# The last layer's gate of an encoder kernel: two blocks of tokens against three, with reloaded weights in another order

## The chip, the cores and the metric

The kernel runs on one core of a Trainium2 chip. The metric is the device time of one execution in microseconds. The engines are named as the profile names them: PE is TensorE (PEld its weight loads), DVE is VectorE, ACT is ScalarE, POOL is GpSimd, and SP issues most DMAs. A line number such as L834 is a line of the kernel before; from line 818 on the changed kernel's numbers are up to two higher.

## What is computed

The reference is a two-layer encoder trunk on 1024 tokens of width 1024. The change touches only the end of the second layer and the final norm:

```python
h = h + jnp.concatenate([y_mla, y_gla], axis=-1) @ w_out[i]
gate = jax.nn.sigmoid(rmsnorm(h, ple_norm[i]) @ w_ple_gate[i])
h = h + gate * (p[i] @ w_ple_proj[i])
...
return rmsnorm(h, final_norm)
```

`rmsnorm` divides by the root of the mean square over the 1024 channels of a token, so the final output of a token needs all channels of its h.

## The kernel before

Activations lie with channels on the 128 partitions and tokens along the row, so h is eight tiles `hs[t]` of 128 channels by 1024 tokens. Every fp32 product is made of three matmuls on split operands (high part times high part, low times high, high times low). The order of the instructions on each engine is fixed at build time by a scheduler; each engine runs its queue in that order and waits where an operand or a buffer is not ready.

**Weights.** `load_split` (L135) brings one half tile (128 x 512) of a weight: SP loads it into `wr` (two buffers), ACT copies it to the high part (L142) and its negative to the low part (L146), and POOL issues a second, accumulating DMA (L147) of the same half onto the low part. `load_w8` (L150) does this for the two halves of one output tile. Its results go to the `wh`/`wl` buffers, five halves of each, or, with `keep`, to tiles `kwh`/`kwl` of their own.

**The gate of the last layer** (L804 to L859) runs over blocks of tokens, `TAIL`, 736 and then 288 tokens. For each block it makes the eight output tiles t one after another. A tile is 24 matmuls for each of its `k` column pieces (L834), into a PSUM tile of tag `mm` or `aux` in turn (two buffers each); then DVE multiplies by `r_h`, the rstd of the gate's norm (L837), ACT takes the sigmoid (L838), SP loads `pj`, the tile of the projected embedding (L840), DVE multiplies by it (L841) and adds the product to h (L843), ACT squares h (L847, or L845 into `acc` for the first tile), and DVE adds the square to `acc` (L849). The weights of tiles 4 to 7 (`KEEP`) are kept from the first block on; those of tiles 0 to 3 are loaded again for the second block, whose order is 0, 1, 2, 3, 4, 5, 6, 7.

**The final norm.** After a block, `rstd` (L170) sums `acc` over the partitions: the split parts `sqh` (ACT, L128) and `sql` (DVE, L129) go through two matmuls with ones (L181), DVE transposes the result (L184), makes the inverse root with small operations (L189 to L197) and transposes back (L201). Then `finish` (L808) scales a tile of h by it (L811) and SP stores it (L812). For the first block the eight finishes are put into `later` and made one after each tile of the second block, through a buffer `fin`; for the last block they stand at the end, in place. `gt` and `fin` share three buffers.

Of the kernel before, what the change touches and what calls it, by code (L numbers as in the profile page):

```python
# [31 lines left out]

T_SMALL, T_GQ, T_GK, T_GV, T_CKV, T_CQ, T_GG, T_GA = 0, 1, 3, 5, 9, 11, 14, 18
N_IN = 22
TAIL = (slice(0, 736), slice(736, 1024))

KEEP = (4, 5, 6, 7)

# [19 lines left out]
def hybrid_encoder(ctx: ExitStack, tc: tile.TileContext, xT, pT, pos, vecs, w_in, wq, wk, wv,  # L58
# [35 lines left out]
    def bank2(tag="mm"):  # L94
        return pp.tile([P, 2, HC], F32, tag=tag, name="ps")

    def on(site):
        return {"P": nc.gpsimd, "V": nc.vector}[ENG[site]]
# [15 lines left out]
    def flat(t):  # L114
        return t.rearrange("p a b -> p (a b)")

    def st(shape=(P, S), dt=F32, name="st"):
        return sp.tile(list(shape), dt, tag="st", name=name)

    def mt(dt=F32, name="mt"):  # L120
        return rp.tile([P, S], dt, tag="r", name=name)
# [9 lines left out]
    def split_gain(hi, lo, src, g):  # L131
        nc.scalar.activation(hi, src, AF.Copy, scale=g)
        nc.vector.scalar_tensor_tensor(lo, src, g, hi.bitcast(F32), op0=ALU.mult, op1=ALU.subtract)
# [16 lines left out]
    def load_w8(src, keep=False):  # L150

        ops = []
        if keep:
            whole = mt(F32R, "kwh"), mt(F32R, "kwl")
        for half in range(2):
            c = slice(half * HC, (half + 1) * HC)
            hi, lo = load_split(src[:, c], HC, [t[:, c] for t in whole] if keep else None)
            ops += [(hi[:, k * P:(k + 1) * P], lo[:, k * P:(k + 1) * P]) for k in range(4)]
        return ops

    def mm3(ps, ws, xs):

        n = len(ws)
        for i, ((wh, wl), (xh, xl)) in enumerate(zip(ws, xs)):
            for j, (a, b) in enumerate(((wh, xh), (wl, xh), (wh, xl))):
                for c in range(2):
                    nc.tensor.matmul(ps[:, c, :], lhsT=a, rhs=b[:, c * HC:(c + 1) * HC],  # L167
                                     start=(i == 0 and j == 0), stop=(i == n - 1 and j == 2))
# [119 lines left out]
    for L in range(DEPTH):  # L288
# [496 lines left out]
        if not last_layer:  # L785
            xs = []
            sq = SquareSum()
            for t in range(8):
                ps = bank2()
                mm3(ps, load_w8(w_gate[L, t]), gh)  # L790
                g = st(name="gt")
                nc.vector.tensor_tensor(g, flat(ps), r_h, op=ALU.mult)
                nc.scalar.activation(g, g, AF.Sigmoid)
                pj = st(name="pj")
                nc.sync.dma_start(pj, projd[L][t])
                on("gate").tensor_tensor(g, g, pj, op=ALU.mult)
                on("hadd").tensor_tensor(hs[t], hs[t], g, op=ALU.add)
                nc.sync.dma_start(h1d[t], hs[t])
                sq.add(hs[t])
                hi, lo = mt(F32R, "xh"), mt(F32R, "xl")  # L800
                g1 = vec[:, V_LAYER * (L + 1) + V_LN + t:V_LAYER * (L + 1) + V_LN + t + 1]
                split_gain(hi, lo, hs[t], g1)
                xs.append((hi, lo))
        else:  # L804

            kept, later = {}, []

            def finish(t, w, r, o=None):  # L808
                hw = hs[t][:, w]
                o = hw if o is None else o[:, :w.stop - w.start]  # L810
                nc.vector.scalar_tensor_tensor(o, hw, vec[:, V_FIN + t:V_FIN + t + 1], r, op0=ALU.mult, op1=ALU.mult)  # L811
                nc.sync.dma_start(outT[t][:, w], o)  # L812

            for w in TAIL:
                n = w.stop - w.start
                k = -(-n // HC)
                m = n // k

                def cut(t):
                    return t.rearrange("p (c m) -> p c m", m=m)  # L820

                last_block = w.stop == S
                acc = mt(name="acc")[:, :n]
                todo = [t for t in range(8) if t not in kept] + list(kept)
                for at, t in enumerate(todo):
                    ps = bank2("aux" if at % 2 else "mm")[:, :k, :m]
                    ws = kept[t] if t in kept else load_w8(w_gate[L, t], t in KEEP)
                    if t in KEEP:
                        kept[t] = ws
                    for i in range(8):  # L830
                        for j, (a, b) in enumerate(((ws[i][0], gh[i][0]), (ws[i][1], gh[i][0]),
                                                    (ws[i][0], gh[i][1]))):
                            for c in range(k):
                                nc.tensor.matmul(ps[:, c, :], lhsT=a, rhs=cut(b[:, w])[:, c, :],  # L834
                                                 start=(i == 0 and j == 0), stop=(i == 7 and j == 2))
                    g = st(name="gt")[:, :n]
                    nc.vector.tensor_tensor(cut(g), ps, cut(r_h[:, w]), op=ALU.mult)  # L837
                    nc.scalar.activation(g, g, AF.Sigmoid)  # L838
                    pj = mt(name="pj")[:, :n]
                    nc.sync.dma_start(pj, projd[L][t][:, w])  # L840
                    nc.vector.tensor_tensor(g, g, pj, op=ALU.mult)  # L841
                    hw = hs[t][:, w]
                    nc.vector.tensor_tensor(hw, hw, g, op=ALU.add)  # L843
                    if at == 0:
                        nc.scalar.activation(acc, hw, AF.Square)  # L845
                    else:
                        nc.scalar.activation(g, hw, AF.Square)  # L847
                        if at < 7 or not last_block:
                            nc.vector.tensor_tensor(acc, acc, g, op=ALU.add)  # L849

                    if later:
                        finish(*later.pop(0), st(name="fin"))
                if last_block:
                    r = rstd((acc, g), D, n=n)
                    for t in todo:
                        finish(t, w, r[:, :n])
                else:
                    r = rstd(acc, D, n=n)
                    later = [(t, w, r[:, :n]) for t in todo]  # L859
# [82 lines left out]
```

## Time and profile before

| | |
|---|---|
| median of 3 runs | 1467.03 us (1465.24 to 1467.93) |
| profiled execution, its own time | 1462.53 us |
| its span, first to last instruction | 1460.8 us |
| mean granted TensorE clock, of full speed | 0.981 |
| PE busy | 1379.5 us, 94% |
| DVE busy | 863.2 us, 59% |
| ACT busy | 720.7 us, 49% |
| POOL busy | 427.7 us, 29% |

The busy shares are means over the whole program. The gate of the last layer fills the last 120 us of the span, from about 1341 us on, and is best read there by windows and timelines. Matmuls overlap: the time that one takes from the next is the distance of their starts, not the duration in its row.

### The profile page before, as it was taken

The numbers are of one execution on the slowest core, as the hardware profiler recorded it, in microseconds if no ns is written. First come the engines' busy times: TensorE is split into PE (matmuls) and PEld (weight loads), VectorE is DVE, ScalarE is ACT, GpSimd is POOL, SyncE is SP. The second block draws the span as 40 slices with busy tenths as digits, with TensorE's granted clock in tenths as the row PEclk, the third lists the DMA queues.
The fourth block names the chain that finished last, engine by engine and source line by source line (L and its number), as shares of the span: only waits on it lengthen the run. The fifth ranks groups of instructions, "written<-read, shape, count | busy, mean of one in ns | idle before, by whom it ended". The sixth has DMA issues, their size and how long they took to land. (4 is left out here: it accounts for less than half of the span.)

```text
span 1460.8 us, 21130 instructions
## 1 busy us (share of the span) xinstructions
PE 1379.5 (94%) x8400; PEld 1168.7 (80%) x8400; DVE 863.2 (59%) x1260; ACT 720.7 (49%) x1013; POOL 427.7 (29%) x312
## 2 busy tenths in 40 slices
PE   7999999999889999999999999889989999999985
PEld 6799778878678788888889877778877888878984
DVE  2576745788446544464455676667744564456547
ACT  6565475545345443364445555534444453346541
POOL 3421211212346454112432111211244564311210
PEclk9999999999999999999999999999999999999997
DMA  7663546345531223256765343334651212335863
GB/s 275 184 131 73 108 106 178 82 100 132 151 61 54 65 73 88 71 108 151 200 163 124 79 88 79 88 74 94 176 144 41 66 51 73 101 80 101 218 135 123
DMA packets 77794, 163.94 MB, mean 112 GB/s; under 512 B 9536, under 2 KB 17088, under 8 KB 77696
## 3 DMA queue, kind: packets, MB, share of 16 engines
q1 hardware_dynamic: 51200, 116.19, 26.0%
q0 software_dynamic: 26496, 46.41, 19.1%
q8 instruction: 66, 1.08, 0.3%
q14 instruction: 32, 0.26, 0.1%
HBM read 128.74 MB, written 25.43 MB: 106 GB/s over the span
## 5 line engine op out<-in xcount | busy, mean ns | idle before, releaser
L146 ACT ACTIVATE wl<-wr 128x512 fp32r<-128x512 f32 (+2 forms) x176 | 107.3, 610 | 311.5 <-PE ps L167 279.3
L675 POOL TENSOR_SCALAR sc<-sc,sums 128x1024 f32<-128x1024 f32 x64 | 182.0, 2856 | 101.7 <-DVE sums L674 83.7
L147 POOL DMA_DIRECT2D wl<-in_w_in x84 | 72.6, 877 | 349.1 <-ACT wl L146 311.3
L142 ACT ACTIVATE wh<-wr 128x512 fp32r<-128x512 f32 (+2 forms) x184 | 110.7, 603 | 34.5 <-PE ps L647 13.2
L673 ACT ACTIVATE sc<-ps,top 128x1024 f32<-128x1024 f32 x64 | 71.4, 1116 | 83.2 <-DVE top L671 72.8
L129 DVE TENSOR_TENSOR el<-ps,eh 128x1024 fp32r<-128x1024 f32 x64 | 78.0, 1221 | 46.8 <-ACT eh L128 45.8
L670 DVE TENSOR_REDUCE top<-ps 128x1 f32<-128x1024 f32 x64 | 78.2, 1222 | 43.3 <-PE ps L667 43.3
L167 PE MATMUL ps<-xh,wh 128*128 128x512 f32 x288 | 92.3, 401 | 8.7 <-DVE gate L362 4.6
L456 DVE SCALAR_TENSOR_TENSOR s<-s,last 64x128 f32<-64x128 f32 x208 | 77.0, 370 | 36.8 <-ACT s L102 29.9
L167 PE MATMUL ps<-x0h,wh 128*128 128x512 f32 x288 | 91.6, 400 | 7.1 <-DVE t L609 4.1
L167 PE MATMUL ps<-x0h,wl 128*128 128x512 f32 x288 | 91.5, 398 | 0.3 <-DMA wl<-in_w_in 0.3
L167 PE MATMUL ps<-xh,wl 128*128 128x512 f32 x288 | 91.4, 396 | 0.0
L167 PE MATMUL ps<-x0l,wh 128*128 128x512 f32 x288 | 91.0, 397 | 0.0
L167 PE MATMUL ps<-xl,wh 128*128 128x512 f32 x288 | 90.8, 395 | 0.0
L167 PE MATMUL ps<-yh,wh 128*128 128x512 f32 x256 | 80.6, 392 | 0.9 <-DVE h L727 0.9
L128 ACT ACTIVATE eh<-ps 128x1024 fp32r<-128x1024 f32 x64 | 65.3, 1021 | 32.1 <-PE ps L688 30.6
L167 PE MATMUL ps<-yl,wh 128*128 128x512 f32 x256 | 79.5, 390 | 0.0
L167 PE MATMUL ps<-yh,wl 128*128 128x512 f32 x256 | 79.4, 391 | 0.0
L147 POOL DMA_DIRECT2D wl<-in_w_out x32 | 27.9, 872 | 169.5 <-ACT wl L146 168.8
L688 PE MATMUL ps<-ident,sc 128*128 128x128 f32 x512 | 66.5, 273 | 6.9 <-DVE ql L129 3.1
L688 PEld LDWEIGHTS ps<-ident,sc 128*128 128x128 f32 x512 | 59.2, 140 | 15.7 <-DVE ql L129 3.6
L167 PEld LDWEIGHTS ps<-xh,wh 128*128 128x128 f32 x288 | 54.4, 192 | 21.3 <-DVE gate L362 5.0
(258 smaller groups left out, 3576.8 us busy)
## 6 DMA issues: line engine op xcount, KB each, us to landing
wr<-in_w_in SPq DMA_DIRECT2D x88, 256.0 KB, 3.4
wl<-in_w_in POOLq DMA_DIRECT2D x84, 256.0 KB, 4.8
wr<-in_w_gate SPq DMA_DIRECT2D x40, 256.0 KB, 3.2
projd<-po SPq DMA_DIRECT2D x16, 512.0 KB, 4.1
wr<-in_w_out SPq DMA_DIRECT2D x32, 256.0 KB, 3.1
wl<-in_w_out POOLq DMA_DIRECT2D x32, 256.0 KB, 4.6
wl<-in_w_gate POOLq DMA_DIRECT2D x32, 256.0 KB, 4.7
xraw<-in_xT SPq DMA_DIRECT2D x8, 512.0 KB, 5.0
```

The lines of the kernel that those rows point to most:

```text
L128: nc.scalar.activation(hi, src, AF.Copy)
L129: nc.vector.tensor_tensor(lo, src, hi.bitcast(F32), op=ALU.subtract)
L142: nc.scalar.activation(hi[:, :n], raw[:, :n], AF.Copy)
L146: nc.scalar.activation(lo[:, :n], raw[:, :n], AF.Copy, scale=-1.0)
L147: nc.gpsimd.dma_start(lo[:, :n], src, accum_op=ALU.add)
L167: nc.tensor.matmul(ps[:, c, :], lhsT=a, rhs=b[:, c * HC:(c + 1) * HC], start=(i == 0 and j == 0), stop=(i == n - 1 and j == 2))
L456: nc.vector.scalar_tensor_tensor(state(n)[rows], state(m)[rows], alpha[rows, m:m + 1], state(n)[rows], op0=ALU.mult, op1=ALU.add)
L670: nc.vector.tensor_reduce(m, flat(ps), axis=AX.X, op=ALU.max, negate=True)
L673: nc.scalar.activation(e, flat(ps), AF.Exp, bias=m, scale=SCALE, accum_out=sums[:, b:b + 1])
L675: nc.gpsimd.tensor_scalar(e, e, sums[:, b:b + 1], None, op0=ALU.mult)
L688: nc.tensor.transpose(out=ps[:, j, b * P:(b + 1) * P], in_=e[:, kt], identity=ident)
```

## The change

There are three blocks of 512, 288 and 224 tokens instead of two of 736 and 288. The first block makes the tiles in the order 0 to 7 and keeps 4 to 7, as before. The second and the third take a kept and a reloaded tile in turn: 4, 0, 5, 1, 6, 2, 7, 3. Tiles 0 to 3 are therefore loaded three times instead of twice, eight half tiles more. The finishes of a block are made one after each tile of the next block (`before` takes over the list `later` of the block ahead), so there are now three rstd chains and 24 finishes instead of two and 16.

```diff
-TAIL = (slice(0, 736), slice(736, 1024))
+TAIL = (slice(0, 512), slice(512, 800), slice(800, 1024))
...
                 n = w.stop - w.start
                 k = -(-n // HC)
                 m = n // k
+                before, later = later, []
...
                 last_block = w.stop == S
                 acc = mt(name="acc")[:, :n]
-                todo = [t for t in range(8) if t not in kept] + list(kept)
+
+                todo = [t for pair in zip(KEEP, range(4)) for t in pair] if kept else list(range(8))
                 for at, t in enumerate(todo):
...
-                    if later:
-                        finish(*later.pop(0), st(name="fin"))
+                    if before:
+                        finish(*before.pop(0), st(name="fin"))
```

ACT's queue in block 1, where the first kept weights are copied (`gt` is the sigmoid's tile, `acc` the first square, `kwh` and `kwl` the two parts of a kept half). Before:

```order
L838 ACT_TABLE_LOAD
L838 ACTIVATE gt<-gt 128x736 x2
L845 ACTIVATE acc<-h 128x736
L142 ACTIVATE kwh<-wr 128x512
L146 ACTIVATE kwl<-wr 128x512
L142 ACTIVATE kwh<-wr 128x512
L146 ACTIVATE kwl<-wr 128x512
```

Now:

```order
L840 ACT_TABLE_LOAD
L840 ACTIVATE gt<-gt 128x512 x3
L847 ACTIVATE acc<-h 128x512
L142 ACTIVATE kwh<-wr 128x512
L146 ACTIVATE kwl<-wr 128x512
L840 ACTIVATE gt<-gt 128x512
L142 ACTIVATE kwh<-wr 128x512
L146 ACTIVATE kwl<-wr 128x512
```

The first kept half stands behind three sigmoids instead of two, and in both behind the first square.

ACT's queue in block 2 of the changed kernel, with buffer numbers. `gt_11747` belongs to its first tile (4), `gt_11797` to its second (0); `wl_12138` and `wl_12145` are the two halves of tile 0 for block 3:

```order
L840 ACTIVATE gt_11747<-gt_11747 128x288
L146 ACTIVATE wl_11944<-wr_11942 128x512
L142 ACTIVATE wh_11943<-wr_11942 128x512
L146 ACTIVATE wl_12025<-wr_12023 128x512
L142 ACTIVATE wh_12024<-wr_12023 128x512
L847 ACTIVATE acc_11721<-h_10737 128x288
L146 ACTIVATE wl_12032<-wr_12030 128x512
L142 ACTIVATE wh_12031<-wr_12030 128x512
L146 ACTIVATE wl_12138<-wr_12136 128x512
L840 ACTIVATE gt_11797<-gt_11797 128x288
L146 ACTIVATE wl_12145<-wr_12143 128x512
L849 ACTIVATE gt_11797<-h_10321 128x288
```

Before, ACT has no weight copy behind the first sigmoid of the last block; now tile 0's sigmoid and its square each stand behind a copy for block 3, which waits for a buffer that TensorE frees.

SP's queue at the end of block 2 of the changed kernel (`wr_12400` and `wr_12407` are the halves of tile 3 for block 3, `pj_12127` is the first pj of block 3):

```order
L141 DMA wr_12319<-in_w_gate 128x512
L141 DMA wr_12400<-in_w_gate 128x512
L812 DMA out_0<-fin_11982 128x512
L812 DMA out_0<-fin_12019 128x512
L812 DMA out_0<-fin_12070 128x512
L141 DMA wr_12407<-in_w_gate 128x512
L842 DMA pj_12127<-projd1_96 128x224
L842 DMA pj_12177<-projd1_96 128x224
L842 DMA pj_12214<-projd1_96 128x224
```

Before, all pj of the last block are issued ahead of the first store; now those of block 3 stand behind the eight stores of block 1's finishes and behind the last reloaded half, which waits for one of the two `wr` buffers.

## Rows read from the trace of the kernel before

**Rows 1.** The page: the span.

```profile
span 1460.8 us, 21130 instructions
```

**Rows 2.** Windows: stretch, length, busy of PE PEld DVE ACT POOL, clock, DMA share, GB/s.

```profile
1380.00:1385.00 5.00, 5.00 (x32) 5.00 (x31) 1.85 (x2) 1.92 (x5) 1.49 (x2) 1.00 1.08 267
1400.00:1405.00 5.00, 5.00 (x32) 5.00 (x31) 3.61 (x4) 1.17 (x3) 0.49 (x1) 1.00 0.78 150
1410.00:1415.00 5.00, 2.55 (x20) 2.32 (x18) 2.83 (x4) 3.69 (x7) 1.73 (x2) 1.00 0.40 81
1415.00:1420.00 5.00, 3.05 (x12) 3.01 (x13) 1.29 (x2) 2.21 (x4) 0.86 (x1) 0.66 1.05 242
1440.00:1445.00 5.00, 0.00 (x0) 0.00 (x0) 4.63 (x12) 1.64 (x4) 0.00 (x0) 0.87 0.39 151
```

**Rows 3.** Timeline of PE at the wait: start, us, instruction, idle before it.

```profile
1412.13 0.29 PE L834 MATMUL ps<-hl,wh 128*128 128x288 f32 x1
1412.26 0.29 PE L834 MATMUL ps<-hh,wh 128*128 128x288 f32 x1
1416.95 0.61 PE L834 MATMUL ps<-hh,wl 128*128 128x288 f32 x1 [4.40 <-DMA wl<-in_w_gate]
...
1419.76 0.41 PE L181 MATMUL ps<-sqh,ones_r 128*128 128x512 f32 x1
```

**Rows 4.** Timeline of DVE in the last block.

```profile
1423.59 0.95 DVE L184 STREAM_TRANSPOSE rstd<-ps 128x736 f32<-128x736 f32 x1 [5.49 <-PE ps L181]
...
1428.66 0.98 DVE L811 SCALAR_TENSOR_TENSOR fin<-h,vec,rstd 128x736 f32<-128x736 f32 x1
...
1448.04 0.46 DVE L843 TENSOR_TENSOR h<-h,gt 128x288 f32<-128x288 f32 x1
```

**Rows 5.** Groups by shape from 1341 on: busy us, mean ns, idle before.

```profile
L811 DVE SCALAR_TENSOR_TENSOR fin<-h,vec,rstd 128x736 f32<-128x736 f32 x8 | 7.8, 981 | 0.1
...
L841 DVE TENSOR_TENSOR gt<-gt,pj 128x736 f32<-128x736 f32 x8 | 7.4, 925 | 10.8 <-ACT gt L838 10.7
...
L841 DVE TENSOR_TENSOR gt<-gt,pj 128x288 f32<-128x288 f32 x8 | 3.6, 453 | 0.3 <-ACT gt L838 0.2
...
L811 DVE SCALAR_TENSOR_TENSOR h<-h,vec,rstd 128x288 f32<-128x288 f32 x8 | 3.5, 510 | 0.0
```

**Rows 6.** Timeline of PE at the end of the output projection.

```profile
1336.13 0.61 PE L167 MATMUL ps<-yh,wh 128*128 128x512 f32 x2
1336.58 0.62 PE L167 MATMUL ps<-yh,wl 128*128 128x512 f32 x2
```

**Rows 7.** Timeline of DVE: the first operation that needs the gate's rstd.

```profile
1359.11 0.92 DVE L837 TENSOR_TENSOR gt<-ps,rstd 128x736 f32<-128x736 f32 x1
```

**Rows 8.** Timeline of ACT: the first copy to a kept buffer.

```profile
1364.91 0.61 ACT L142 ACTIVATE kwh<-wr 128x512 fp32r<-128x512 f32 x1
```

**Rows 9.** Timeline of POOL: the first accumulating DMA onto a kept half.

```profile
1366.33 0.86 POOL L147 DMA_DIRECT2D kwl<-in_w_gate  x1 [8.15 <-ACT kwl L146]
```

**Rows 10.** DMA issues from 1340 to 1420: count, KB, median us to landing.

```profile
wr<-in_w_gate SPq DMA_DIRECT2D x18, 256.0 KB, 4.1
...
kwl<-in_w_gate POOLq DMA_DIRECT2D x8, 256.0 KB, 5.9
pj<-projd SPq DMA_DIRECT2D x6, 144.0 KB, 5.5
```

**Rows 11.** DMAs onto kwl.

```profile
DMA to landing us min/median/max: 5.0/5.9/7.0
```

**Rows 12.** DMAs onto pj, 736 and 288 columns.

```profile
DMA to landing us min/median/max: 2.3/5.3/6.6
```

**Rows 13.** Timeline of PE: sum matmuls of 224 columns.

```profile
1423.18 0.27 PE L181 MATMUL ps<-sqh,ones_r 128*128 128x224 f32 x1
1423.28 0.27 PE L181 MATMUL ps<-sql,ones_r 128*128 128x224 f32 x1
```

**Rows 14.** Timeline: the final scaling, eight instructions.

```profile
1453.88 3.52 DVE L811 SCALAR_TENSOR_TENSOR h<-h,vec,rstd 128x288 f32<-128x288 f32 x8
```

## The prediction, made blind

> **What bounds the kernel now.** I took the span from the page [rows 1] and then read a table of five-microsecond windows over the last layer's gate [rows 2], then the timelines of the engines there. The windows show three stretches. From 1340 on TensorE is busy all 5.00 us of each of the thirteen windows up to 1405: that is block 1 (736 tokens), bound by matmuls. At 1410 to 1415 it is busy for 2.55 us of 5 and the rest is a wait. After 1440 it does no gate matmul at all, while the program still has 20 us to run. The wait is in [rows 3]: the matmul at 1412.26 is followed by one at 1416.95, which waited for a reloaded weight half. The restart runs at the lower of the two clocks, 1.2 GHz (granted 0.66 over that window): eleven matmuls fill 1416.95 to 1419.76, 2.8 us instead of 11 x 0.133 = 1.5, so 1.3 us more are lost. What ends last, however, is VectorE [rows 4]: its first "fin" starts at 1428.66, once block 1's rstd is ready, and its last addition to h ends at 1448.50, 19.84 us later. The grouped rows [rows 5] say that these 19.84 us are full: eight "fin" of 0.981 (7.8) and 27 operations of 288 columns at 0.453 (12.2) make 20.0 us. So the end of the program stands on a chain: block 1's last weight, block 1's rstd, VectorE's backlog, the last rstd, the last eight stores. A change pays if it shortens that chain, not if it fills TensorE.
>
> **The change, term by term.** All on the profiled execution: span 1460.8, time 1462.53; it lies 4.5 us under the median of the runs shown, 1467.03, to which the difference is added at the end.
>
> *TensorE work.* The columns stay 1024 per weight column group, and the count of matmuls too. A 512-column matmul costs 0.227 us (two in 0.45 us, [rows 6]), a 288-column one 0.133 [rows 3]. A 224-column one with its own weight load does not occur; the bounds are 0.10 (a 224-column matmul to the next with weights that don't change value, [rows 13]) and 0.133; I take 0.107, and it turns out not to matter.
>
> *Step 1, block 1 stalls at its first kept tile.* Tiles 0 to 3 now take 96 x 0.227 and four 512-column sums between them, 0.9: from 1341.6, where the last matmuls of the output projection end, to 1364.3. Tile 4 goes to the kept buffers. ACT copies its weights behind the sigmoids of tiles 0 to 2 and the first square, and these hang on rstd, ready at 1359.11 [rows 7], which the change does not move. Before, 5.80 us pass from there to the first kept copy at 1364.91 [rows 8]; with 512 columns in place of 736 on the three VectorE and the ACT operations between, about 1.05 us less, so 1363.9. The accumulating DMA is issued 1.42 us after the copy begins [rows 8, 9] and lands 5.9 later (5.0 to 7.0, [rows 10, 11]): 1371.2. TensorE waits 6.9 us, longer than the 4.4 of [rows 3], and I add the 1.3 us of low clock seen there. Tiles 4 to 7 then take 21.8: block 1 ends at **1394.3**. The weights keep up: before, the kept halves came one per 3 us, and the last would be there 2 us before it is used.
>
> The Trainium skill ("DMA: Bandwidth & Descriptors", section "Anatomy of one DMA — SWDGE (gpsimd) path") gives such a DMA 2.0 us plus its bytes over 436 GB/s, 2.6 us for 256 KB, and by that the half would land at 1367.9 and the wait be 3.6 us. No accumulating DMA of these rows is that fast, 5.0 at least [rows 11], so the measurement decides.
>
> *Step 2, block 1's sum.* From its last matmul eight dependent operations of 512 columns (five VectorE at 0.688, interpolated between 0.453 and 0.925 in [rows 5]; three ACT at 0.61, [rows 8]) with the last matmul's drain and small gaps between give 5.9 us: 1400.2. TensorE has by then done kept tiles 4 and 5 of block 2 (6.4 us, 1400.7) and takes the first sum matmul, 18 matmuls of tile 0, the second: 1403.6. Transpose to first fin was 5.07 us [rows 4]; two transposes of 512 instead of 736 save 0.5. First fin at **1408.2**, 20.5 us earlier than before.
>
> *Step 3, VectorE in block 2.* Eight fins of 512 columns (0.981 - 0.925 + 0.688 = 0.744) and 28 operations at 0.453: 6.0 + 12.7 = 18.7 us, gapless as in [rows 5]. New are waits on ACT. In its queue the sigmoid of tile 0 stands behind a copy of block 3's first weight half, which needs the buffer that tile 1 frees on TensorE at 1410.3 (1403.6, then 0.8 + 2.7 + 3.2); the sigmoid is done at 1411.2, VectorE was ready at 1410.1: 1.1 us. The square of tile 0 stands behind the next copy, which needs tile 2's first half (1412.4 on TensorE) and a raw half that lands 4.1 us [rows 10] after a copy at 1409.8, so 1413.9; the square is done at 1415.0, VectorE was ready at 1412.1: 2.9 us. Bounds for both together: 0 and, with raw halves that land as late as the slow pj of [rows 10], 5.5 us, about 6. VectorE ends block 2 at 1408.2 + 18.7 + 4.0 = **1430.9**.
>
> *Step 4, an rstd that before does not exist.* The square's high part on ACT takes at most the 0.61 of [rows 8]; for 288 columns I take 0.5: 1431.4. TensorE, which has finished two tiles of block 3, waits at that sum in its own queue; then sum, 21 matmuls of 224, sum: 2.7 us, 1434.1. Transpose to first fin, 5.07 - 2 x 0.47 = 4.1 us, would give 1438.2. Inside that chain VectorE multiplies by the first pj of block 3, at about 1435.6. SP issues this pj behind the last reloaded half, which waits for a buffer that ACT empties only after the sigmoid of block 3's first tile (1432.6) and two copies (1433.8); pj is issued at 1434.2. It lands 2.3 to 6.6 us later [rows 12]; the median of the 288-column ones, 5.5 [rows 10], came from a burst beside weight loads, and here one half is in flight; I take 3.5, 1437.7. Wait 2.1 us (bounds 0.9 and 5.2). First fin of block 2 at 1440.3.
>
> *Step 5, VectorE in block 3, and the end.* 27 operations at 0.453 - 64 x 0.00105 = 0.386 and eight fins of 288 columns at 0.510 [rows 5]: 10.4 + 4.1 = 14.5, so 1454.8. From there the program took 1448.50 to 1460.8 = 12.3 us; the eight final fins shrink from 3.52 [rows 14] to 3.0, transposes and square by 0.2: 11.6. End at **1466.4**, that is 5.6 us later than 1460.8. The removed wait of [rows 3] (4.4 + 1.3) is inside: kept and reloaded tiles alternate, and reloaded halves have 6.4 us per tile pair in block 2. It is bought with the wait of step 1, which is larger, and with step 4.
>
> TensorE does not set this end: 1394.3 + 25.6 + 20.5 + 0.8 = 1441.2 without waits, 13 us before VectorE. The sixteen reloaded halves of blocks 2 and 3 cost ACT 16 x 2 x 0.61 = 20 us, spread over 47 us; their place in its queue is what steps 3 and 4 price.
>
> Sum: 1467.0 + 5.6 = **1472.6**. With the low bounds together (ACT waits 0, pj 2.3, kept half 5.0) 1472.6 - 4.0 - 1.2 - 0.9 = 1466.5, with the high ones (+2.0, +3.1, +1.1) 1478.8.
>
> **The rivals.** What a measurement of this kernel can tell from no change is about 0.2%, 2.9 us.
>
> *No change.* The waits on ACT and pj of steps 3 and 4 don't occur, because raw halves and pj land early: 5.6 - 4.0 - 2.1 = -0.5, so 1466.5. For it: [rows 4, 5] show no such wait before, and DMA has room after 1400. Against: the order of ACT and SP. By the price of the Trainium skill in step 1 the time would be 3.3 us below the forecast, 1469.3, which is no change too; the rows give that little weight.
>
> *Faster: TensorE sets the end.* VectorE's back-to-back operations overlap a little: in [rows 4, 5] 20.0 us of work stand in 19.84, waits included. If 55 short operations each start 0.08 us early and no wait of steps 3 and 4 occurs, VectorE follows within a tile of TensorE's 1441.2, adds the last tile's chain (about 2 us) and 11.6: 1454.8, that is 6.0 faster, 1461.0. It decides if VectorE's backlog at the last gate matmul is under 3 us; now it is over 8, since no gate matmul runs after 1440 and the last addition ends at 1448.50. Against it: two rstd chains that VectorE must sit through.
>
> *Slower still: transfers.* At 1380 to 1385 the DMA engines are busy all the time [rows 2]. If eight more reloads and sixteen early stores hold them there through block 3, with raw landings of 5.5, accumulations of 7.0 and pj of 6.6, step 1 grows by 1.1, step 3 by 2.0 and step 4 by 3.1: 5.6 + 6.2 = 11.8 us, 1478.8. For it also: 1.05 at 1415 to 1420. Against: the windows before and after, at 0.40 and 0.39.
>
> **How the numbers follow.** Forecast 0.48, transfers 0.13, no change 0.25, TensorE 0.14. The forecast's own lower bound lies within 0.2%, which the chance for no change takes in. So slower 0.61, same 0.25, faster 0.14. The range leaves out half of the fast rival and half of the slowest one: 1461.5 to 1478.5.
>
> **What would show it.** TensorE should wait some 7 us near 1364 for a kept half, and none for a reloaded one in block 2; the first fin should start near 1408 and the last addition end near 1455; a sum matmul in block 3 should hold TensorE for 2 us or more; VectorE's first product of block 3 should wait for pj. I am wrong if block 1 runs through without that wait, or if the last addition ends less than 4 us after the last gate matmul.

## The result and the profile after

The changed kernel takes 1487.98 us (median of 5 runs, 1485.62 to 1493.38) against 1465.96 of the kernel before (5 runs, 1463.06 to 1467.93): ratio 1.0154, 95% interval 1.0135 to 1.0173. It is 22.0 us slower. The prediction had slower, but by 5.6 us, and its range ended at 1478.5.

The profiled execution after took 1493.38 us, 5.4 above its median, and the one before 1462.53, 3.4 below its own. The two traces are therefore some 31 us apart where the medians are 22.0 apart, and what is read from them adds up to more than the 22. The span after, from the page, which answers to [rows 1]:

```profile
span 1491.4 us, 21314 instructions
```

To compare executions I cut the end of the program in two: A, from the gate's first matmul to the first final scaling of block 1 (the first L811 on VectorE), and B, from there to the end of the span. Before, A was 1428.66 - 1341.57 = 87.1 us and B 32.1. The forecast was A 66.6 (1408.2) and B 58.2 (1466.4). After, the gate starts at 1344.26, the first scaling at 1423.09: A is 78.8 and B 68.3. So A missed by 12.2 us and B by 10.1, together 22.3, where by the medians 16.4 (22.0 less 5.6) are to be explained.

The windows of five microseconds after, with the columns of [rows 2], show where TensorE stands idle:

```profile
1370.00:1375.00 5.00, 0.36 (x2) 0.29 (x1) 3.52 (x6) 3.08 (x6) 1.73 (x2) 0.89 0.76 157
...
1380.00:1385.00 5.00, 5.00 (x22) 4.06 (x21) 0.69 (x1) 1.57 (x3) 1.00 (x2) 0.93 1.01 228
1400.00:1405.00 5.00, 3.46 (x27) 3.23 (x26) 1.29 (x2) 3.03 (x6) 0.86 (x1) 1.00 0.89 191
1405.00:1410.00 5.00, 2.52 (x20) 2.29 (x18) 3.16 (x5) 1.58 (x3) 0.89 (x1) 1.00 0.79 162
1410.00:1415.00 5.00, 1.96 (x7) 1.87 (x8) 2.65 (x5) 1.70 (x3) 0.00 (x0) 0.65 0.03 7
1415.00:1420.00 5.00, 5.00 (x28) 4.94 (x27) 1.32 (x5) 1.95 (x4) 0.87 (x1) 0.67 0.27 59
1425.00:1430.00 5.00, 3.78 (x29) 3.54 (x27) 0.92 (x2) 2.18 (x5) 1.06 (x2) 1.00 1.05 307
```

The first row is the stall at the first kept tile, which was forecast. The rows at 1400 to 1420 show a stall that was not: TensorE runs dry while block 1 is being summed, and after a wait of 5.5 us it comes back at the lower clock, 1.2 GHz (granted 0.65 and 0.67 in these windows). At 1425 VectorE, which should be the busiest engine there, works 0.92 us of 5.

TensorE's waits after, grouped (us in total, times, longest); before, the wait of [rows 3] stood here:

```profile
PE ps L836 <- DVE gt L839: 9.5, 4, 3.1
PE ps L181 <- ACT sqh L128: 7.9, 2, 5.5
PE ps L836 <- ACT kwh L142: 5.6, 2, 4.6
PE ps L181 <- DVE acc L851: 3.9, 1, 3.9
PE ps L836 <- DMA wl<-in_w_gate: 1.1, 1, 1.1
```

No wait for a reloaded half is left in blocks 2 and 3; the 1.1 us falls in block 1. TensorE waits for VectorE to empty PSUM (L839), for the sum's high part (`sqh`) and for the high parts of kept halves (`kwh`).

**Why block 1's sum is late.** ACT's timeline, from block 1's last tiles to its sum:

```profile
1392.93 0.63 ACT L142 ACTIVATE wh<-wr 128x512 fp32r<-128x512 f32 x1 [2.95 <-DMA wr<-in_w_gate]
...
1396.78 0.63 ACT L142 ACTIVATE wh<-wr 128x512 fp32r<-128x512 f32 x1 [0.18 <-DMA wr<-in_w_gate]
1397.32 0.62 ACT L146 ACTIVATE wl<-wr 128x512 fp32r<-128x512 f32 x1
1401.04 0.63 ACT L142 ACTIVATE wh<-wr 128x512 fp32r<-128x512 f32 x1 [3.10 <-DMA wr<-in_w_gate]
1401.58 0.61 ACT L146 ACTIVATE wl<-wr 128x512 fp32r<-128x512 f32 x1
1402.10 0.61 ACT L849 ACTIVATE gt<-h 128x512 f32<-128x512 f32 x1
1403.64 0.63 ACT L142 ACTIVATE wh<-wr 128x512 fp32r<-128x512 f32 x1 [0.93 <-DMA wr<-in_w_gate]
1404.18 0.61 ACT L146 ACTIVATE wl<-wr 128x512 fp32r<-128x512 f32 x1
1404.70 0.62 ACT L840 ACTIVATE gt<-gt 128x512 f32<-128x512 f32 x1
...
1412.35 0.63 ACT L128 ACTIVATE sqh<-acc 128x512 fp32r<-128x512 f32 x1 [0.76 <-DVE acc L851]
```

The copies of block 2's reloaded halves stand between block 1's squares (L849) and sigmoids (L840), and each waits for a raw half: 3.10 us at 1401.04 and 0.93 at 1403.64, with the square of 1402.10 and the sigmoid of 1404.70 behind them. VectorE waits behind these, and TensorE begins block 1's last matmul long before the sum:

```profile
1396.63 0.69 DVE L843 TENSOR_TENSOR gt<-gt,pj 128x512 f32<-128x512 f32 x1 [5.32 <-ACT gt L840]
...
1402.74 0.69 DVE L851 TENSOR_TENSOR acc<-acc,gt 128x512 f32<-128x512 f32 x1 [4.70 <-ACT gt L849]
```

```profile
1399.01 0.39 PE L836 MATMUL ps<-hl,kwh 128*128 128x512 f32 x1
```

The last tiles of block 1 then go through VectorE and ACT one behind the other, and `sqh` comes at 1412.35, 13.3 us after that matmul began. The raw halves come one by one because SP may ask for the next only when ACT has emptied one of two buffers; SP's timeline has this as one long row:

```profile
1386.45 18.70 SPq L141 DMA_DIRECT2D wr<-in_w_gate  x7
1405.24 0.39 SPq L842 DMA_DIRECT2D pj<-projd  x1
```

Seven issues take SP 18.7 us, and the first `pj` of block 2 waits behind them.

**Why block 2 is slow.** VectorE's timeline after the first scaling:

```profile
1425.99 0.46 DVE L843 TENSOR_TENSOR gt<-gt,pj 128x288 f32<-128x288 f32 x1 [1.12 <-ACT gt L840]
...
1430.30 0.46 DVE L851 TENSOR_TENSOR acc<-acc,gt 128x288 f32<-128x288 f32 x1 [3.35 <-ACT gt L849]
1431.09 0.46 DVE L839 TENSOR_TENSOR gt<-ps,rstd 128x288 f32<-128x288 f32 x1 [0.33 <-DMA out<-fin]
...
1441.59 0.46 DVE L839 TENSOR_TENSOR gt<-ps,rstd 128x288 f32<-128x288 f32 x1 [1.55 <-DMA out<-fin]
1443.25 0.75 DVE L811 SCALAR_TENSOR_TENSOR fin<-h,vec,rstd 128x512 f32<-128x512 f32 x1 [0.84 <-DMA out<-fin]
1448.52 0.46 DVE L839 TENSOR_TENSOR gt<-ps,rstd 128x288 f32<-128x288 f32 x1 [0.99 <-DMA out<-fin]
```

The two waits on ACT are those that were forecast (1.1 and 2.9 us). The waits on `out<-fin` are not: `gt` and `fin` take turns in three buffers, a `fin` holds its buffer until its store has landed, and the eviction of PSUM (L839), which needs a new `gt`, waits for it. In block 2 VectorE waits so for 2.9 us on L839 and 0.8 on L811, and in block 3 for 1.8 more on L839. TensorE in turn waits for the eviction, but only in part because of stores: of the 9.5 us above, 3.1 (at 1445.53) stand mostly behind these stores, 2.8 (1431.60) mostly behind the square that VectorE awaited until 1430.30, 2.0 (1464.64) behind the first `pj` of block 3 and 1.5 (1404.09) behind block 1's late tail. The stores are late beside the transfers around them; e4 below shows them without. From issue to landing in the stretch 1385 to 1470 (KB each, median us):

```profile
wr<-in_w_gate SPq DMA_DIRECT2D x16, 256.0 KB, 5.1
wl<-in_w_gate POOLq DMA_DIRECT2D x16, 256.0 KB, 5.4
out<-fin SPq DMA_DIRECT2D x8, 256.0 KB, 4.6
```

### The profile page after: what moved, and what is told of

Read it like the earlier page. It is cut to its first block, busy times and chain, and to the rows that moved or that the text cites. A ratio compares the mean times of both kernels' runs of the same rounds, so it can differ in the third digit from the quotient of the medians.

```text
span 1491.4 us, 21314 instructions
## 1 busy us (share of the span) xinstructions
PE 1389.9 (93%) x8400; PEld 1170.1 (78%) x8400; DVE 870.2 (58%) x1314; ACT 732.7 (49%) x1046; POOL 434.6 (29%) x320
## 5 line engine op out<-in xcount | busy, mean ns | idle before, releaser
L146 ACT ACTIVATE wl<-wr 128x512 fp32r<-128x512 f32 (+2 forms) x184 | 112.4, 611 | 319.1 <-PE ps L167 277.2
L142 ACT ACTIVATE wh<-wr 128x512 fp32r<-128x512 f32 (+2 forms) x192 | 115.5, 604 | 36.8 <-PE ps L647 13.2
L128 ACT ACTIVATE eh<-ps 128x1024 fp32r<-128x1024 f32 x64 | 65.3, 1022 | 32.2 <-PE ps L688 30.6
L147 POOL DMA_DIRECT2D wl<-in_w_gate x40 | 34.6, 864 | 137.6 <-ACT wl L146 135.1
```

Source lines behind the costliest of these rows:

```text
L128: nc.scalar.activation(hi, src, AF.Copy)
L142: nc.scalar.activation(hi[:, :n], raw[:, :n], AF.Copy)
L146: nc.scalar.activation(lo[:, :n], raw[:, :n], AF.Copy, scale=-1.0)
L147: nc.gpsimd.dma_start(lo[:, :n], src, accum_op=ALU.add)
```

## Experiments

Ratios are to the kernel before, measured beside it. A and B are from the one profiled execution of each, the gate's start taken from its own trace; single executions differ by a few microseconds (the one after lies 5.4 above its median, that of e10 4.6 below), so they show where, and the ratios how much. Where scalings are in place, the first of them can stand later in VectorE's queue, and A and B shift against each other.

| run | ratio (95% interval) | A | B |
|---|---|---|---|
| before | 1 | 87.1 | 32.1 |
| changed kernel | 1.0154 (1.0135 to 1.0173) | 78.8 | 68.3 |
| e1 scalings in place | 1.0094 (1.0076 to 1.0111) | 81.2 | 53.7 |
| e2 two blocks, new order | 1.0003 (0.9988 to 1.0018) | | |
| e3 three blocks, old order | 1.0180 (1.0161 to 1.0199) | 82.1 | 60.8 |
| e4 no reloads | 1.0002 (0.9990 to 1.0014) | 66.9 | 53.0 |
| e5 before, in place | 0.9986 (0.9969 to 1.0004) | | |
| e6 more raw buffers | 1.0182 (1.0156 to 1.0209) | 65.0 | 82.6 |
| e7 the same, in place | 1.0142 (1.0117 to 1.0167) | 64.6 | 77.9 |
| e8 no reloads, in place | 0.9963 (0.9947 to 0.9979) | 69.5 | 45.2 |
| e10 copies on GpSimd | 1.0140 (1.0109 to 1.0170) | 70.4 | 66.2 |
| e11 GpSimd subtracts | 1.0085 (1.0068 to 1.0102) | 71.3 | 58.6 |
| e13 the same, in place | 1.0064 (1.0042 to 1.0086) | 78.4 | 50.6 |
| e14 before, GpSimd subtracts | 0.9966 (0.9953 to 0.9980) | 83.7 | 32.2 |
| e15 the same, in place | 0.9964 (0.9947 to 0.9981) | | |
| e16 half the reloads | 1.0087 (1.0062 to 1.0111) | 76.7 | 57.1 |

**e1, scalings in place.**

```diff
-                        finish(*before.pop(0), st(name="fin"))
+                        finish(*before.pop(0))
```

> The change with one part taken away: the finishes of blocks 1 and 2 are written in place onto h, as the last block's are, so they need no buffer of the three that the sigmoid's tile shares. Theory S (VectorE waits for stores to leave those buffers: 4.7 + 0.8 us before gate products and fins in the changed kernel's trace, and TensorE behind it for PSUM, 2.8 + 3.1 + 2.0): 5 to 9 us faster than the change, about 1480. Theory Q (ACT copies reloaded weights in front of the evacuation and waits for their raw halves): under 2 us, 1486 to 1488, since ACT's queue stays as it is.

About 9 us of the 22 come back, and all of it in B: the first scaling is as late as after, and VectorE's waits no longer name a store.

**e2 and e3, each half of the change alone.** e2 keeps two blocks and takes the order of turns; e3 keeps three blocks and the old order.

```diff
-TAIL = (slice(0, 512), slice(512, 800), slice(800, 1024))
+TAIL = (slice(0, 736), slice(736, 1024))
```

> The change's order alone: two blocks of 736 and 288 tokens as before, the second in the order 4, 0, 5, 1, 6, 2, 7, 3. No added reload, no third rstd. If the alternating order is worth what it was costed at (the 4.4 us wait for a reloaded half and 1.3 us of low clock), VectorE's backlog still ends the program, so I expect 1462 to 1466, no slower than before. If the order of ACT's queue is what hurts (theory Q), it should be slower than before here too, by 3 us or more, since the reload copies move among the last block's sigmoids.

```diff
-                todo = [t for pair in zip(KEEP, range(4)) for t in pair] if kept else list(range(8))
+                todo = [t for t in range(8) if t not in kept] + list(kept)
```

> The change's three blocks alone: 512, 288, 224, each later block in the old order, the four reloaded tiles first. Four reloaded tiles in a row need a half every 1.6 us in block 2 and 1.3 in block 3, while halves came one per 3 us: some 5 + 6 us more of waits than with taking turns, 1493 to 1500. If instead the reloads are not what sets the pace (theory S, stores and buffers), it is the same as the change within 3 us.

The order alone can't be told from no change, though it removes the wait of [rows 3]. In three blocks, the old order is about 4 us slower than turns (1.0180 against 1.0154, the intervals overlap), which falls between the two expectations, and its TensorE waits 9.2 us for `wl` after 1396. The third block with its reloads costs, not the order.

**e4, no reloads.**

```diff
-                    ws = kept[t] if t in kept else load_w8(w_gate[L, t], t in KEEP)
+                    ws = kept[t] if t in kept else kept[t + 4] if kept and w.start else load_w8(w_gate[L, t], t in KEEP)
```

> The change without any reload: blocks 2 and 3 use the kept weights of tile t + 4 where tile t was reloaded, so that part of the gate's products is made with other weights and 16 half loads (raw load, two ACT copies, accumulating DMA) are gone. Block 1 keeps its 16. Theory Q and transfers: the time falls by 15 us or more, below the kernel before, to 1455 to 1465; what then remains above TensorE's pace is step 1 (the wait of some 5 us for the first kept half). Theory S: stores and the shared buffers still pace VectorE, 1478 or more.

Without reloads, three blocks cost nothing: 1.0002. A is 66.9 us, within 0.3 of the forecast's 66.6. ACT's timeline in that run has no copy between block 1's last operations, and `sqh` comes 4.7 us after block 1's last matmul began, where it took 13.3 after:

```profile
1396.03 0.63 ACT L840 ACTIVATE gt<-gt 128x512 f32<-128x512 f32 x1 [2.54 <-DVE gt L839]
1398.14 0.63 ACT L849 ACTIVATE gt<-h 128x512 f32<-128x512 f32 x1 [1.49 <-DVE h L845]
1399.53 0.63 ACT L128 ACTIVATE sqh<-acc 128x512 fp32r<-128x512 f32 x1 [0.76 <-DVE acc L851]
```

```profile
1394.81 0.39 PE L836 MATMUL ps<-hl,kwh 128*128 128x512 f32 x1
```

The stores land in less than half the time (issue to landing, 1385 to 1470):

```profile
out<-fin SPq DMA_DIRECT2D x8, 256.0 KB, 2.0
```

So the whole cost hangs on the reloads. The next runs ask through which door.

**e5 and e8, controls to e1.** The edit of e1 on the kernel before, and on e4.

> The kernel before, two blocks as it stands, with the first block's final scaling written over the block's own tokens in place of a buffer of its own. It is the control to the same edit on the changed kernel, which there gave back about 9 of the 22 us. Theory S (the stores hold the three shared buffers because the reloads' transfers make them land late): in the kernel before the reloads' transfers are over when the second block's scalings begin, so the stores are short and the edit gives 0 to 3 us, ratio 0.998 to 1.000. If the buffers are short in any case, whatever the transfers: 5 us or more, ratio below 0.997.

> The changed kernel without any reload (the second and third block's tiles 0 to 3 use the kept weights of tiles 4 to 7, so these four tiles of the output's last layer are computed with other weights), and with the final scalings in place. Without reloads alone the run was level with the kernel before, and in place alone gave back 9 us. Theory S with late stores only where reloads run: the stores land in 2 us there, so nothing is left to give, 0 to 3 us, ratio 0.998 to 1.000. If the shared buffers hold the second block whatever the transfers: 5 us or more below the kernel before, ratio below 0.997.

On the kernel before the edit can't be told from no change. Without reloads it gives 0.4% (1.0002 to 0.9963), some 6 us, where Theory S had 0 to 3. So S holds only in part: in three blocks the shared buffers hold VectorE even with stores of 2 us (in e4 it waits 2.9 us for them on L839), and whether the late stores make more of it (9 against 6) lies within the intervals.

**e6, more raw buffers.** In blocks 2 and 3 each raw half gets a tile of the large pool, so the copies come to stand behind block 1's sum.

```diff
-        raw = wp.tile([P, HC], F32, tag="wr", name="wr", bufs=BUFS[2])
+        raw = wp.tile([P, HC], F32, tag="wr", name="wr", bufs=BUFS[2]) if src_raw is None else src_raw
...
-            hi, lo = load_split(src[:, c], HC, [t[:, c] for t in whole] if keep else None)
+            hi, lo = load_split(src[:, c], HC, [t[:, c] for t in whole] if keep else None, mt(name="wr")[:, :HC] if wide else None)
```

> The changed kernel; in the second and third block the raw halves of the weights have a buffer each from the large pool, in place of the two that they share. In the queues, all of the reloads' copies on ScalarE now stand behind the first block's sum of squares. Theory Q (ScalarE's queue: copies that wait for a raw half stand in front of the sigmoids and squares of the first block): the first block's sum ends as early as without reloads, its first final scaling is near 1409 in place of 1423, and the run gains 6 to 13 us, ratio to the kernel before 1.006 to 1.011. Theory V (the reloads' transfers themselves, wherever the copies stand): the weights of the second block come as late or later, the gain at the sum is lost at the first reloaded tile, ratio 1.013 to 1.018.

A falls to 65.0, a little below the forecast's 66.6; B grows to 82.6 and the run is no better than the changed kernel. TensorE's timeline shows where the gain went: it now waits for the reloaded halves themselves, and after the longest wait it comes back slow (0.61 us for a matmul that behind the other waits shows 0.40; granted clock 0.63 from 1410 to 1415):

```profile
1409.31 0.40 PE L836 MATMUL ps<-hh,wh 128*128 128x288 f32 x1 [1.68 <-ACT wh L142]
1413.21 0.61 PE L836 MATMUL ps<-hh,wl 128*128 128x288 f32 x1 [3.51 <-DMA wl<-in_w_gate]
```

From 1404 on these waits sum to 12.7 us for `wl` (eight of them) and 4.0 for `wh` (four). The copies hurt block 1 where they stood, but standing later they are late for block 2.

**e10, the copies on GpSimd.** Transfers and buffers as they were.

```diff
-        nc.scalar.activation(hi[:, :n], raw[:, :n], AF.Copy)
+        nc.gpsimd.tensor_copy(hi[:, :n], raw[:, :n]) if pool else nc.scalar.activation(hi[:, :n], raw[:, :n], AF.Copy)
...
-            nc.scalar.activation(lo[:, :n], raw[:, :n], AF.Copy, scale=-1.0)
+            nc.gpsimd.tensor_scalar(lo[:, :n], raw[:, :n], -1.0, None, op0=ALU.mult) if pool else nc.scalar.activation(lo[:, :n], raw[:, :n], AF.Copy, scale=-1.0)
```

> The changed kernel with the reloads' two copies of each raw half in the second and third block on GpSimd in place of ScalarE; transfers, bytes and buffers as they were. Theory Q: ScalarE's queue holds the gate's work alone, the first block's sum ends about when it does without reloads, first final scaling near 1409 to 1412 in place of 1423, and the run gains 6 to 13 us, ratio to the kernel before 1.006 to 1.011, less what slower copies on GpSimd cost the reloaded tiles. Theory V: the same transfers in the same stretch hold pj, the stores and the raw halves as before, ratio 1.013 to 1.018 or above.

A is 70.4, 8.5 us less than after, yet the run gains nearly nothing. It is not a clean test, though: VectorE slowed down beside the copies (its 288-column product L843 took 0.555 us on average, 0.456 in e4; the last section shows the like in e13), and now GpSimd waits for the raw halves, 19.1 us after 1395.

**e11, e13 and e14, half the transfers.** The reloads' low halves are raw minus high, by GpSimd, without the negated copy on ACT and without the accumulating transfer. e13 adds the edit of e1; e14 is the kernel before with the same.

```diff
-        if first[0]:
+        if first[0] or pool:
             nc.gpsimd.tensor_tensor(lo[:, :n], raw[:, :n], hi[:, :n].bitcast(F32), op=ALU.subtract)
...
-                    ws = kept[t] if t in kept else load_w8(w_gate[L, t], t in KEEP)
+                    ws = kept[t] if t in kept else load_w8(w_gate[L, t], t in KEEP, w.start > 0)
```

> The changed kernel with the reloads' low halves made by a GpSimd subtraction (raw minus high) in place of ScalarE's negated copy and the accumulating transfer: the second and third block read each reloaded half from memory once, not twice; ScalarE keeps one copy of a half, the two raw buffers stay. Two runs so far cleared the first block's sum of the reloads' copies and gained little at the end, so Theory V (the reloads' transfers and their number) is now ahead: the 16 accumulating transfers were 35% of the DMA engines' time in the stretch 1385 to 1470, and without them the run gains 8 to 18 us, ratio to the kernel before 1.003 to 1.010. Theory R (two raw buffers: a half is only asked for when an older one has been copied, so the halves come one after the other whatever the transfers carry): the raw buffer is now held longer, by GpSimd's 1.3 us after ScalarE's copy, and nothing is gained, 1.012 or above.

> The kernel of the run before with the final scalings in place as well. Theory V: once the transfers are halved the stores land in 2 to 3 us and the shared buffers hold little, so in place gives 2 to 5 us more where alone it gave 9; ratio to the kernel before 0.998 to 1.006, level with the run without reloads and in place (0.996) or a little above. If the two costs are independent of one another: the full 9 us more.

> The kernel before, two blocks, with its one set of reloads made by the GpSimd subtraction. It is the control: Theory V says that in two blocks the reloads come under the first block's 78 us of matmuls and cost the end little, so ratio 0.997 to 1.001; if the accumulating transfers cost the same per set wherever they stand, half of what the changed kernel gains here is gained too, 0.993 to 0.997.

e11 gives back 0.7%, some 10 us, in A and in B. In e11's trace a store of 256 KB lands in 2.1 us and a raw half in 2.6 (medians, 1385 to 1470), against 4.6 and 5.1 after. The edit also takes one of the two copies of each half out of ACT's queue, so the run does not show what the transfers alone are worth. e13 can't be told from e11, though 9 us more were possible if the two costs were independent: with stores that land fast, in place gave about 3. e13 stays above e8 by 1%. Two of its windows have VectorE busy throughout:

```profile
1420.00:1425.00 5.00, 5.00 (x40) 5.00 (x39) 5.00 (x9) 2.15 (x4) 2.26 (x2) 1.00 0.78 273
1425.00:1430.00 5.00, 4.06 (x34) 3.83 (x33) 5.00 (x9) 1.92 (x5) 2.28 (x2) 1.00 0.92 296
```

e14, the control, is faster than the kernel before by 0.34%: there one set of reloads is made, and the wait of [rows 3] for `wl` is gone, since no accumulating transfer stands in front of it. Its ratio of 0.9966 lies just outside what V allowed (0.997 to 1.001) and inside what the other reading did (0.993 to 0.997): one set of reloads here gives back half of what two sets do in e11, as if a set cost the same wherever it stands. Its interval (0.9953 to 0.9980) reaches into both.

**e16, half the reloads.** As e4, for tiles 2 and 3 alone.

```diff
+                    ws = kept[t] if t in kept else kept[t + 4] if kept and w.start and t > 1 else load_w8(w_gate[L, t], t in KEEP)
```

> The changed kernel with two of the four reloads in each of the second and third block (tiles 2 and 3 use the kept weights of tiles 6 and 7, so these two tiles of the last layer are computed with other weights). With 16 reloaded halves the change costs 22 us, with none 0 to 1. Theory V in proportion to the transfers: 9 to 13 us, ratio 1.006 to 1.009. A threshold (the reloads cost only what they are late; half of them come in time between the kept tiles): 0 to 6 us, ratio 1.000 to 1.004. Theory Q alone (one copy waiting for its raw half in front of the first block's last squares is enough): 15 us or more, ratio above 1.010.

0.87% of 1463.4 is 12.7 us, somewhat over half of the 22, and no threshold of 0 to 6 us. But the two parts don't share the gain alike: B falls to 57.1, four above e4, with stores that land in 2.0 us again, while A stays at 76.7, ten above e4. In ACT's queue the copies of the same number of reloaded halves, five, stand before block 1's sum as after (1390.68 to 1401.07 here, 1392.93 to 1403.64 after), and `sqh` comes 11.4 us after block 1's last matmul began (1398.37):

```profile
1401.07 0.63 ACT L142 ACTIVATE wh<-wr 128x512 fp32r<-128x512 f32 x1 [0.38 <-DMA wr<-in_w_gate]
...
1409.78 0.63 ACT L128 ACTIVATE sqh<-acc 128x512 fp32r<-128x512 f32 x1 [0.76 <-DVE acc L851]
```

So the proportion of the whole is no proportion of its parts: for A the first copies are enough, as theory Q has it (its 1.010 lies inside the interval, which ends at 1.0111).

**e7, e6 in place.**

> The changed kernel with a buffer for each raw half of the reloads, as in the run with more raw buffers, and with the final scalings in place. If the stores' buffers are what ate the first block's 15 us there (theory S): the gains show together, ratio 1.000 to 1.006. If it is the weights that then come late, behind pj and the stores (theory V): the second block still waits for reloaded halves, ratio 1.010 to 1.016.

1.0142: the earlier sum is not eaten by the stores' buffers but by the weights, which still come late (TensorE waits 11.7 us for `wl` after 1396, 4.7 for `wh`).

**e15, the kernel before with both edits.**

> The kernel before, two blocks, with both edits: the reloads' low halves by a GpSimd subtraction (alone 0.9966) and the first block's scalings in place (alone 0.9986, not told from no change). If they add: 0.994 to 0.996, faster than both kernels. If the subtraction has taken the late stores away already: 0.996 to 0.998, as without in place.

0.9964: in place adds nothing that can be told, though the interval (0.9947 to 0.9981) takes in the 0.995 that adding would give. e14 and e15 beat both kernels, by some 5 us the one before and by some 28 the changed one.

## Why the prediction was wrong

Its sign was right and its size was not: 5.6 us were forecast, 22.0 measured.

*Step 1* was right, in its reason too, with one term too small. TensorE was to restart at 1371.2; it does at 1371.00 in e4 and at 1374.66 after, where the gate began 2.7 us later. TensorE and its weight loads after:

```profile
1369.51 0.51 PE L836 MATMUL ps<-hh,kwh 128*128 128x512 f32 x1 [0.93 <-ACT kwh L142]
1374.66 0.80 PE L836 MATMUL ps<-hh,kwh 128*128 128x512 f32 x1 [4.64 <-ACT kwh L142]
1375.21 0.29 PEld L836 LDWEIGHTS ps<-hh,kwl 128*128 128x128 f32 x1 [0.27 <-DMA kwl<-in_w_gate]
```

The longer wait ends with the copy of the third kept half (ACT, 1373.97 to 1374.60), which waited for its raw half. The low half that the step named came no earlier: the weight load at 1375.21 still waited for its accumulating transfer, issued at 1370.27. Too small was the price of the lower clock, put at 1.3 us: from the restart to the end of block 1 e4 took 24.0 us (1371.00 to 1395.04, its last matmul's start and 0.23), 2.2 more than the 21.8 of work.

*Step 2* failed, at "eight dependent operations of 512 columns ... give 5.9 us". That prices the chain as if its engines were free. ACT's was not: the reloads' copies of block 2 stand in it between block 1's squares, each behind a raw half. The prediction read ACT's queue at the first kept copies (step 1) and in block 2 (step 3), and not at block 1's end, where these copies stand. Counted as the step counts, from the last matmul's start and 0.23 to the end of `sql`, the chain took 5.9 us in e4 (1395.04 to 1400.89) and 14.5 after (1399.24 to 1413.71). With the copies gone (e4) or behind the sum (e6), A is 66.9 and 65.0 against the 66.6 forecast; with them it was 78.8. Of the 12.2 us that A missed by, the chain is 8.6. Some 2 more are TensorE's slow restart behind the late sum: from the first sum matmul to the second it took 4.9 us after (1413.04 to 1417.95) and 2.6 in e4 (1401.36 to 1403.95, granted clock 1.00). The rest is mostly block 1's later end.

*Step 3* failed, at "gapless as in [rows 5]". Its 4.0 us of ACT waits were about right where it had them (1.12 and 3.35 above); 2.7 more stood elsewhere (0.88, 1.29 and 0.51). Missing were the waits for the buffers of `gt` and `fin` behind a store, 2.9 us on L839 and 0.8 on L811. Before, the stores of block 1, 368 KB each, land in 2.3 us at the median and one set of reloads is over; here those of 256 KB land in 4.6 beside the second. VectorE's block 2 was to take 22.7 us, from the first scaling to its end, and took 28.9 (1423.09 to 1451.95). e1 puts the price of the shared buffers at 9 us, more than the 5.5 of waits that name a store, and by e8 some 6 of them need no reload at all; no step and no rival named this mechanism.

*Step 4* had the wait for `pj` right: 2.1 us were forecast and 2.8 measured, behind the last reloaded half as said:

```profile
1461.30 0.39 DVE L843 TENSOR_TENSOR gt<-gt,pj 128x224 f32<-128x224 f32 x1 [2.81 <-DMA pj<-projd]
```

The step as a whole took 11.8 us (1451.95 to 1463.77) in place of 9.4. Behind a wait of 2.39 us for `sqh` TensorE ran the matmuls between the two sums partly at the lower clock (granted 0.74 from 1450 to 1455): from the first sum to the second it took 4.15 us (1452.48 to 1456.63), where 2.7 had been put for both sums and all between.

*Step 5*'s 14.5 us for block 3 became 15.9 (1463.8 to 1479.65); its end chain of 11.6 took 11.75.

Of the rivals, the slowest, *transfers*, was the nearest, and it too was 9 us short (1478.8), since it only made each landing slower in the steps that stood. It did not ask what a late raw half or a late store holds back in a queue or a buffer.

Of its signs, a stall of TensorE at a kept half, none at a reloaded one in block 2, the sum matmul in block 3 that holds TensorE for over 2 us and the wait for `pj` came; the first "fin" near 1408 and the last addition near 1455 did not (1423.09 and 1479.65). Neither of its two signs of being wrong showed, for both watched for a faster end.

What is shown: the cost is the reloads' (e4). In A it is the copies in front of block 1's sum (e4, e6, e16), and moving them does not cure the whole, since the weights are then late (e6, e7). In B it is the shared buffers (e1) and the second half of the reloads (e16). e11 gives back nearly half, but it halves the transfers and ACT's copies in one edit. What stays open is the rest of e13, about 1% over e8. VectorE's slower operations beside GpSimd's, the copies that remain in ACT's queue (the chain of step 2 takes 9.6 us there, 1396.47 to 1406.08) and the raw halves' two buffers can each have a part in it, and no run separates them.

## What to carry to other kernels

A block more of tokens means a set of reloads more. Price it not by its busy time but by what stands behind its copies in the queue of each engine that carries the chain, and look at the end of the block before as well as at the new one. Where a tile that a store reads shares its buffers with the tiles that empty PSUM, a slow store can become a wait of the engine that empties PSUM, and of TensorE behind it. And moving a copy that waits for a transfer only helps if the transfer is not needed soon after: here the wait moved with it.

## What the runs showed of the hardware

GpSimd's elementwise work slowed VectorE. In e13, GpSimd subtracts from 1415.85 to 1417.17 and from 1417.43 to 1418.72; VectorE's timeline beside it (a 16-column operation before takes 0.17 us, the 288-column product 0.45):

```profile
1415.57 0.46 DVE L845 TENSOR_TENSOR h<-h,gt 128x288 f32<-128x288 f32 x1
1415.94 1.27 DVE L197 SCALAR_TENSOR_TENSOR nwy<-nwt,nwy 128x16 f32<-128x16 f32 x1
1417.24 0.71 DVE L201 STREAM_TRANSPOSE rstd<-nwy 128x512 f32<-128x512 f32 x1
1417.88 1.16 DVE L843 TENSOR_TENSOR gt<-gt,pj 128x288 f32<-128x288 f32 x1
```

Both slow operations (1.27 and 1.16 us) begin inside a subtraction and end after it. The same group by shape, in e13 and in e4 (busy us, mean ns):

```profile
L843 DVE TENSOR_TENSOR gt<-gt,pj 128x288 f32<-128x288 f32 x7 | 4.9, 702 | 0.0
```

```profile
L843 DVE TENSOR_TENSOR gt<-gt,pj 128x288 f32<-128x288 f32 x7 | 3.2, 456 | 0.7 <-ACT gt L840 0.6
```

The Trainium skill ("SBUF — State Buffer", section "SBUF: two separate sides") says that a VectorE operation with two SBUF inputs and a GpSimd operation that reads SBUF take one port pair in turn, each for its whole instruction. The trace agrees: a product held until the subtraction ends is what 1.16 us in place of 0.45 shows, and the eviction L839, which reads PSUM and one SBUF tile, keeps 0.446 us in e13 against 0.454 in e4; three of them begin inside a subtraction and take 0.45 to 0.46.

A transfer's landing time was set by its company more than by its size: a 256 KB store took 2.0 us at the median without reloads, 4.6 beside them, and 2.1 when they read each half once; before, one of 368 KB took 2.3.
